# Up products grouped by width, a new first stage and a new last stage in a two-layer encoder kernel

## The chip, the cores and the metric

The kernel runs on one core of a Trainium2 chip. The metric is device time in microseconds (us) from the start to the end of one execution. Three runs of the kernel before gave a median of 789.08 us (788.89 to 789.4).

## The reference, cut to what matters

The input is x, 256 tokens by 1024 channels, and there are two layers. Each layer does this:

```
xn = rms_norm(x);  h = xn @ w_in                  # 6176 columns
ya = conv_module(...)       # "glu" columns: gated unit, depthwise conv of 31 taps, LayerNorm, swish
yb = gla_branch(...)        # "gvl": values and low-rank gates; "qk"; "gr"
yc = attention_branch(...)  # "att": windowed attention with rotary and a sink
yd = pool_branch(...)       # "pin": mean pooling of widths 2, 4, 8, 16
merged = sum_n sigmoid(gate_n) * (y_n @ w_branch_n)
x = x + merged @ w_out
x = x + square(relu(rms_norm(x) @ w_ffn_up)) @ w_ffn_down     # 1024 -> 4096 -> 1024
...
return rms_norm(x, final_norm_g)
```

The norms are not applied ahead of the products. Each channel's gain is multiplied into x when it is split, and the token's factor R (one over the root mean square) is multiplied in behind the products, when their sums are read.

## The kernel before, in words

All products run with operands of type float32r, and each operand is split in two parts, hi and lo, so that hi*hi + hi*lo + lo*hi gives nearly full precision. So one product of the reference is three matrix products.

**Weights.** They come in pieces of at most 128 x 1024 numbers (512 KB), in the order that `layer_loads` writes out. `fetch(i)` issues a piece's transfer into one of three `raw` buffers, on the queue of SyncE (SP). `split_w(i)` makes hi with a cast on ScalarE (ACT, L285) and lo with a subtraction on VectorE (DVE, L286), into one of five `hi` and five `lo` buffers. A raw buffer comes free when both have read it. `look_ahead` fetches up to seven pieces and splits up to four pieces ahead of the one in use.

**Order.** A planner (the tile framework's scheduler) puts each engine's instructions in a fixed order when the kernel is built. `urgent()` and `critical()` raise the priority of what stands in them; `after(t)` and `tc.issue_after(t.ins)` hold instructions back until `t` stands in the order. Each engine then works through its list in that order.

**First stage, layer 0.** x arrives with channels on partitions, in four pairs of channel tiles (256 KB each), in turn with the first four weight pieces, all on SP (L933 to L938). `split_x` makes hi (ACT, L437) and lo (DVE, L438) of each channel tile. The first products are `gvl` (8 channel tiles by 288 columns, two token tiles, 48 products of 288 columns), then `glu1` and `glu0` (96 products of 256 columns), then `qk`. `Stats` squares x and sums it, and `st.finish` makes R, which `gla_in` needs to read the `gvl` sums out of their two PSUM banks. `WARM` products on a tile of ones stand ahead of all.

**MLP.** `up(c)` makes 256 hidden channels: for each of 8 channel tiles and two halves t it issues a product of 512 columns (hi weights by x's hi and lo side by side, L1158) and one of 256 columns (lo weights by x's hi, L1159). `down(c)` multiplies the hidden channels back, 24 products of 512 columns (L329 to L331). `up(c)` and `down(c - 1)` take turns, and 16 blocks of each make a layer.

**Layer switch.** When the last two blocks of `down` have made the first half of the channels (h = 0), `add_mlp` adds it to x (DVE, L1210). `turn_x` turns x with PE transposes (L447) and splits it for the next layer's products.

**Last stage, layer 1.** When a token tile `it` is complete, its sum of squares gives one over the root, o and e, and `dg` is that factor on a diagonal (L1279). `normed(it)` multiplies x by the diagonal, which turns and scales it at once (L1244, 8 products of 128 columns in full float32, two passes each), multiplies by the final gain (L1245 on DVE, L1248 on ACT) and sends it out in two transfers.

Of the kernel before, what the change touches and what calls it, by code (L numbers as in the profile page):

```python
# [30 lines left out]
GVL_CUTS = (((0, 2), (2, 4), (4, 6), (6, 8)), ((0, 1), (1, 3), (3, 6), (6, 8)))  # L31
CONV_V = 18
WARM = 14
# [17 lines left out]
def layer_loads(first):  # L51
# [17 lines left out]
    for i, (a, b) in enumerate(cuts):  # L69
        if not first and a == 4:  # L70
            cols256("glu1", C_GLU + 256, (0,))
            cols256("glu0", C_GLU, (0,))
        add(("gvl", i), "w_in", a, b, gvl)
    if first:
        cols256("glu1", C_GLU + 256)
        cols256("glu0", C_GLU)
    else:
        cols256("glu1", C_GLU + 256, (1,))
        cols256("glu0", C_GLU, (1,))
# [47 lines left out]
def cst_layout():  # L127
    off = 0
    for name, n in (("ident", 128), ("band", 256), ("lev", 160), ("rope", 32), ("cnt", 512), ("o64", 128)):
        CST[name] = (off, n)  # L130
        off += n
    return off
# [40 lines left out]
def trunk_kernel(ctx: ExitStack, tc: tile.TileContext, x, w, prm, wup, poolw, cst, out, depth, dbg=None):  # L173
# [49 lines left out]
    cst_t = sb.tile([P, NCST], F32, name="cst_t")  # L223
# [5 lines left out]
    ident = cs("ident")  # L229
# [40 lines left out]
    def fetch(i):  # L270
# [4 lines left out]
        raws[i] = r  # L275
        return d

    def split_w(i):
# [5 lines left out]
        with urgent():  # L284
            a = S.copy(h[:, :n], r[:, :n])  # L285
            V.tensor_tensor(lo[:, :n], r[:, :n], h[:, :n].bitcast(F32), ALU.subtract)  # L286
# [22 lines left out]
    nc.scalar.dma_start(prm_t, prm)  # L309
# [617 lines left out]
    for l in range(depth):  # L927
        if l == 0:
# [4 lines left out]
            for f in range(4):  # L933
                nc.sync.dma_start(xT[:, 2 * f : 2 * f + 2, :], x[:, 2 * f : 2 * f + 2, :])
                sent = fetch(f)
                last = split_w(f)
                for t in (2 * f, 2 * f + 1):
                    split_x(xh[:, t, :], xl[:, t, :], xT[:, t, :], gain0[:, t : t + 1])  # L938
            state["raw"] = state["next"] = 4
            st = Stats()  # L940
            for f in range(4):
                with urgent(), tc.issue_after(last.ins):
                    st.add(f, xT)
# [3 lines left out]
        if l == 0:  # L947
            state["raw"] = 5
            with tc.issue_after(fetch(4).ins):
                nc.sync.dma_start(cst_t, cst)  # L950
            G.tensor_copy(o64r, o64)
        (nc.sync if l else nc.scalar).dma_start(wup_t, wup[:, l * 256 : l * 256 + 256])
        nc.sync.dma_start(poolw_t, poolw[:, l * 256 : l * 256 + 256])
# [18 lines left out]

        cuts = list(enumerate(GVL_CUTS[l == 0]))
        for i, (k0, k1) in cuts if l == 0 else cuts[:2]:
# [4 lines left out]
        ps_g, ps_a = mmt(), None  # L979
        if l:  # L980
            ps_a = mmt()
# [13 lines left out]
        for i in range(2) if l == 0 else (1,):  # L995
            part256(ps_g, "glu1", i)
        if l == 0:
            ps_a = mmt()
        for i in range(2) if l == 0 else (1,):
            done = part256(ps_a, "glu0", i)  # L1000
# [144 lines left out]
        ups = {}  # L1145

        def up(c, parts=(0, 1)):
# [3 lines left out]
            for i in parts:  # L1151
                wh, wl = piece(l, (("up", c), i))
                for k in range(4):
                    f = fx[i][:, k]
                    for t in range(2):
                        w1 = slice(t * P, (t + 1) * P)
                        first, last = i + k == 0, (i, k) == (1, 3)
                        mm(ps[t], wh[:, k, w1], f, start=first, stop=False, skip_group_check=True)  # L1158
                        done = mm(  # L1159
                            ps[t][:, 0, :], wl[:, k, w1], f[:, 0, :], start=False, stop=last, skip_group_check=True  # L1160
                        )
            if 1 not in parts:
# [12 lines left out]
            hid[c] = (hh, hl)  # L1175

# [11 lines left out]

        for i in range(2):
            for c in range(2):  # L1190
                with after(turned if (i, c) == (0, 1) else None):
                    done = up(c, (i,))
                if (i, c) == (0, 0):
                    turned = turn_x(f_parts, 1, col(l, 8, 8), done)
# [18 lines left out]
        if nxt < depth:  # L1213
# [6 lines left out]
            for h in range(2):  # L1220
                for c in (14, 15):
                    with after(turned if (c, h) == (15, 1) else None):
                        done = down(c, (0, 1), (h,))
                    if (c, h) == (14, 1):
                        turned = turn_x(x_parts, 0, col(nxt, 0, 8), done)
# [5 lines left out]
        else:  # L1231
# [4 lines left out]
            def normed(it):  # L1236

                with urgent():
                    for h in range(2):
                        ps = mmt((P, 4, P))  # L1240
                        yo = gh_p.tile([P, 4, P], F32, tag="gh", name=nm("yo"))
                        for t in range(4):
                            c = (4 * h + t) * P
                            mm(ps[:, t, :], xt[:, it, c : c + P], dgs[it], start=True, stop=True)  # L1244
                        V.tensor_tensor(yo[:, :2], ps[:, :2], gb[:, 4 * h : 4 * h + 2], ALU.mult)  # L1245
                        for t in (2, 3):
                            kt = 4 * h + t
                            S.activation(yo[:, t, :], ps[:, t, :], AF.Copy, scale=g[:, kt : kt + 1])  # L1248
                        (nc.sync, nc.scalar)[h].dma_start(
                            out[:, 4 * h : 4 * h + 4, it * P : (it + 1) * P], yo  # L1250
                        )

            dgs = []
            for it in range(2):
                for h in range(2):
                    for c in (14, 15):
                        done = down(c, (it,), (h,))
                    if (it, h) == (1, 0):
                        with tc.issue_after(done.ins):
# [103 lines left out]
```

## Time and profile before

| | |
|---|---|
| median of 3 runs | 789.08 us (788.89 to 789.4) |
| the profiled execution's own time | 788.53 us |
| its span, first to last instruction | 786.7 us |
| PE (TensorE) busy | 773.7 us, 98%, 4298 matrix products |
| DVE busy | 585.3 us, 74% |
| ACT busy | 476.0 us, 61% |
| moved by DMA | 138.49 MB, mean 176 GB/s |

A busy PE is not a PE at its peak: the records of consecutive products overlap, so that the distance from one product's start to the next one's start (its pitch) tells what a product costs. The 1.83 us between the span and the execution's own time lie around the span and are not touched by the kernel's order.

### The profile page before, as it was taken

Reading aid. Unit: us, or ns where it says so; the run is one execution under the profiler, and the core shown is the slowest. Engines: PE = TensorE matmul, PEld = TensorE weight load, DVE = VectorE, ACT = ScalarE, POOL = GpSimd, SP = SyncE. Lnnn points to the kernel's source line nnn. Section 1 sums busy time; section 2 is a strip of 40 time slices with the busy share of each in tenths; the row PEclk is TensorE's granted clock in tenths of the full one; section 3 lists DMA queues with packets and bytes.
Section 4 is the critical chain, followed back from the end, with each engine's and each line's share of the span. In section 5 each row is a group of like instructions: output and inputs, shape, how many; then the busy total and the mean of one; then the engine's idle time right before and its main releaser. Section 6 shows DMA issues by size and latency. Waiting matters only on the chain.

```text
span 786.7 us, 11413 instructions
## 1 busy us (share of the span) xinstructions
PE 773.7 (98%) x4298; PEld 657.8 (84%) x4298; DVE 585.3 (74%) x863; ACT 476.0 (61%) x740; POOL 9.7 (1%) x22
## 2 busy tenths in 40 slices
PE   8999999999999999999999999999999999999996
PEld 7998888888888888888799988788888888888885
DVE  6789999888676666666677999978776766666653
ACT  6788895854564444444568787858545644444443
POOL 2000000000000000000000000000000000000000
PEclk9999999999999999999999999999999999999999
DMA  8755545455556555555465564346655576665631
GB/s 282 234 167 174 176 138 157 140 190 179 188 165 207 191 188 188 190 187 192 141 190 182 161 211 159 108 135 165 209 171 178 165 212 189 190 192 191 193 113 53
DMA packets 41126, 138.49 MB, mean 176 GB/s; under 512 B 4528, under 2 KB 7280, under 8 KB 41072
## 3 DMA queue, kind: packets, MB, share of 16 engines
q1 hardware_dynamic: 39616, 137.05, 55.1%
q10 hardware_dynamic: 1456, 0.73, 0.3%
q8 instruction: 33, 0.54, 0.3%
q14 instruction: 21, 0.17, 0.1%
HBM read 136.71 MB, written 1.05 MB: 175 GB/s over the span
## 4 chain that ended last, share of the span: by engine, by line
PE 95%; DVE 2%; DMA 1%; issue 1%; ACT 1%; DVEq 0%
PE mm L1158 15%; PE mm L329 11%; PE mm L330 10%; PE mm L331 10%; PE ax L331 9%; PE ax L329 9%; PE ax L330 9%; PE mm L1159 8%; PE mm L322 2%; PE mm L321 2%; PE mm L320 2%; PE ax L661 1%; PE ax L822 1%; PE ax L447 1%; DMA raw<-in_w_dram 1%
## 5 line engine op out<-in xcount | busy, mean ns | idle before, releaser
L286 DVE TENSOR_TENSOR lo<-raw,hi 128x1024 fp32r<-128x1024 f32 (+2 forms) x260 | 314.5, 1209 | 139.3 <-ACT hi L285 137.7
L285 ACT CAST hi<-raw 128x1024 fp32r<-128x1024 f32 (+2 forms) x260 | 269.6, 1038 | 210.1 <-issue 53.8
L1158 PE MATMUL mm<-fx,hi 128*128 128x512 f32 x512 | 181.9, 398 | 0.0
L1159 PE MATMUL mm<-fx,lo 128*128 128x256 f32 x512 | 143.1, 281 | 0.0
L329 PE MATMUL mm<-hi,xh 128*128 128x512 f32 (+1 forms) x320 | 122.1, 384 | 1.0 <-ACT hi L285 1.0
L330 PE MATMUL mm<-lo,xh 128*128 128x512 f32 (+1 forms) x320 | 122.3, 383 | 0.4 <-DVE lo L286 0.4
L331 PE MATMUL mm<-hi,xl 128*128 128x512 f32 (+1 forms) x320 | 120.6, 381 | 0.0
L1158 PEld LDWEIGHTS mm<-fx,hi 128*128 128x128 f32 x512 | 96.0, 188 | 23.2 <-DVE fx L438 0.3
L329 PE MATMUL ax<-hi,hh 128*128 128x512 f32 x256 | 100.0, 391 | 0.0
L330 PE MATMUL ax<-lo,hh 128*128 128x512 f32 x256 | 99.9, 390 | 0.0
L1159 PEld LDWEIGHTS mm<-fx,lo 128*128 128x128 f32 x512 | 96.6, 189 | 1.8 <-DVE lo L286 0.3
L331 PE MATMUL ax<-hi,hl 128*128 128x512 f32 x256 | 97.1, 389 | 0.0
L329 PEld LDWEIGHTS mm<-hi,xh 128*128 128x128 f32 x320 | 59.8, 188 | 12.5 <-ACT hi L285 1.2
L330 PEld LDWEIGHTS mm<-lo,xh 128*128 128x128 f32 x320 | 60.1, 188 | 11.3 <-DVE lo L286 0.8
L331 PEld LDWEIGHTS mm<-hi,xl 128*128 128x128 f32 x320 | 60.1, 188 | 11.1
L329 PEld LDWEIGHTS ax<-hi,hh 128*128 128x128 f32 x256 | 48.0, 188 | 10.6
L331 PEld LDWEIGHTS ax<-hi,hl 128*128 128x128 f32 x256 | 48.1, 188 | 10.2
L330 PEld LDWEIGHTS ax<-lo,hh 128*128 128x128 f32 x256 | 48.1, 188 | 8.9
L1170 ACT COPY t<-mm 128x256 f32<-128x256 f32 x64 | 23.4, 370 | 46.0 <-PE mm L1159 46.0
L322 PE MATMUL mm<-xh,lo 128*128 128x256 f32 x160 | 45.5, 284 | 1.0 <-DVE lo L286 1.0
L321 PE MATMUL mm<-xl,hi 128*128 128x256 f32 x160 | 45.4, 284 | 0.0
L320 PE MATMUL mm<-xh,hi 128*128 128x256 f32 x160 | 45.2, 284 | 0.0
(264 smaller groups left out, 983.3 us busy)
## 6 DMA issues: line engine op xcount, KB each, us to landing
raw<-in_w_dram SPq DMA_DIRECT2D x252, 512.0 KB, 3.6
raw<-in_w_dram SPq DMA_DIRECT2D x6, 288.0 KB, 3.2
xT<-in_x_dram SPq DMA_DIRECT2D x4, 256.0 KB, 4.5
cst_t<-in_cst_dram SPq DMA_DIRECT2D x1, 608.0 KB, 5.2
out_dram<-yo SPq DMA_DIRECT2D x2, 256.0 KB, 2.4
out_dram<-yo ACTq DMA_DIRECT2D x2, 256.0 KB, 2.4
raw<-in_w_dram SPq DMA_DIRECT2D x1, 432.0 KB, 4.3
poolw_t<-in_poolw_dram SPq DMA_DIRECT2D x2, 128.0 KB, 4.6
```

What stands on the lines that cost most here:

```text
L285: a = S.copy(h[:, :n], r[:, :n])
L286: V.tensor_tensor(lo[:, :n], r[:, :n], h[:, :n].bitcast(F32), ALU.subtract)
L320: mm(o, a, xh[:, kx, :], start=start, stop=False, skip_group_check=True)
L321: mm(o, a, xl[:, kx, :], start=False, stop=False, skip_group_check=True)
L322: return mm(o, b, xh[:, kx, :], start=False, stop=stop, skip_group_check=True)
L329: mm(o, xh[:, kx, tk], wh[:, k, :], start=start, stop=False)
L330: mm(o, xh[:, kx, tk], wl[:, k, :], start=False, stop=False)
L331: return mm(o, xl[:, kx, tk], wh[:, k, :], start=False, stop=stop)
L447: last = nc.tensor.transpose(ps[:, t, it * P : (it + 1) * P], src[:, it, c : c + P], ident)
L1158: mm(ps[t], wh[:, k, w1], f, start=first, stop=False, skip_group_check=True)
L1159: done = mm(ps[t][:, 0, :], wl[:, k, w1], f[:, 0, :], start=False, stop=last, skip_group_check=True)
L1170: S.copy(z[:, t, :], ps[t][:, 1, :])
```

## The change

Four places are changed.

1. **Up products.** In `up`, the two products of 512 columns of a channel tile now stand together, and then the two of 256 columns. `up` also returns its last product, and the first four part blocks of `up` in a layer are chained in order with `after`.
2. **First stage.** `gvl` comes in pieces of 1, 1, 2, 3 and 1 channel tiles, and `glu` comes in pieces of two channel tiles by 512 columns; the products take turns (gvl 0, gvl 1, glu 0, gvl 2, glu 1, gvl 3, gvl 4, then glu 2 and glu 3 behind R's users). x's first pair comes on SP with pieces 0, 1 and 2; the second pair is issued on ACT's queue behind the cast of piece 1, the third and the fourth behind the cast of piece 4. The `glu` piece 0 is split in two halves. `WARM` goes from 14 to 11. The identity becomes a tile of its own, fetched with `prm_t` and `wup_t` behind piece 5; the other constants and `poolw_t` come later still.
3. **Layer switch.** The first `turn_x` for the next layer stands behind half of the last `down` block (the first token tile) instead of ahead of all of it, and the other half stands behind the transposes.
4. **Last stage.** x is turned by plain transposes against the identity (`turned_out`) and multiplied by the gain when it is read out; the token factor comes as a row from one product of ones with `dg` and is multiplied in afterwards (`normed`). Token tile 0's transposes stand between the `down` products of token tile 1. Token tile 1 goes out in four transfers on two queues.

```
 def split_w(i, cuts=1):
...
+            for c in range(cuts):
+                p = slice(c * n // cuts, (c + 1) * n // cuts)
+                a = S.copy(h[:, p], r[:, p])
+                V.tensor_tensor(lo[:, p], r[:, p], h[:, p].bitcast(F32), ALU.subtract)
...
-            for f in range(4):
-                nc.sync.dma_start(xT[:, 2 * f : 2 * f + 2, :], x[:, 2 * f : 2 * f + 2, :])
-                sent = fetch(f)
-                last = split_w(f)
-                for t in (2 * f, 2 * f + 1):
-                    split_x(xh[:, t, :], xl[:, t, :], xT[:, t, :], gain0[:, t : t + 1])
-            state["raw"] = state["next"] = 4
+            sent = last = None
+            for f, pieces in enumerate(((0, 1, 2), (3, 4), (), ())):
+                with after(last if f >= 2 else sent), critical():
+                    (nc.scalar if f else nc.sync).dma_start(
+                        xT[:, 2 * f : 2 * f + 2, :], x[:, 2 * f : 2 * f + 2, :]
+                    )
+                tiles = (2 * f, 2 * f + 1)
+                for i in pieces:
+                    fetch(i)
+                    if i == 0:
+                        split_x(xh[:, 0, :], xl[:, 0, :], xT[:, 0, :], gain0[:, 0:1])
+                        sent = split_w(0)
+                        split_x(xh[:, 1, :], xl[:, 1, :], xT[:, 1, :], gain0[:, 1:2])
+                        continue
+                    if i == pieces[0]:
+                        for t in tiles:
+                            split_x(xh[:, t, :], xl[:, t, :], xT[:, t, :], gain0[:, t : t + 1])
+                    last = split_w(i, 2 if i == 2 else 1)
+                    if i != 2:
+                        sent = last
+                if not pieces:
+                    for t in tiles:
+                        with tc.issue_after(sent.ins):
+                            split_x(xh[:, t, :], xl[:, t, :], xT[:, t, :], gain0[:, t : t + 1])
+            state["next"] = 5
...
-            with tc.issue_after(fetch(4).ins):
-                nc.sync.dma_start(cst_t, cst)
+            with tc.issue_after(fetch(5).ins):
+                nc.sync.dma_start(ident, cst[:, CST["ident"][0] :])
+                nc.sync.dma_start(prm_t, prm)
+                nc.sync.dma_start(wup_t, wup[:, :256])
...
+        if l == 0:
+            ps_g, ps_a = mmt(), mmt()
+            for i, (k0, k1) in cuts:
+                gvl(i, k0, k1)
+                if i in (1, 2):
+                    glu(i - 1)
...
         if l == 0:
-            ps_a = mmt()
+            for i in (2, 3):
+                done = glu(i)
+            with tc.issue_after(state["dma"].ins):
+                nc.sync.dma_start(cst_t, cst[:, : NCST - P])
+                nc.sync.dma_start(poolw_t, poolw[:, :256])
...
                     for t in range(2):
                         w1 = slice(t * P, (t + 1) * P)
-                        first, last = i + k == 0, (i, k) == (1, 3)
                         mm(ps[t], wh[:, k, w1], f, start=first, stop=False, skip_group_check=True)
+                    for t in range(2):
+                        w1 = slice(t * P, (t + 1) * P)
                         done = mm(
                             ps[t][:, 0, :], wl[:, k, w1], f[:, 0, :], start=False, stop=last, skip_group_check=True
                         )
...
+                done = down(14, (0, 1), (h,))
+                if h == 0:
+                    down(15, (0, 1), (h,))
+                else:
+                    with after(done):
+                        done = down(15, (0,), (h,))
+                    turned = turn_x(x_parts, 0, col(nxt, 0, 8), done)
+                    with after(turned):
+                        down(15, (1,), (h,))
...
+            def turned_out(it, h, behind=None):
+                ps = mmt((P, 4, P))
+                yo = gh_p.tile([P, 4, P], F32, tag="gh", name=nm("yo"))
+                for t in range(4):
+                    c = (4 * h + t) * P
+                    last = nc.tensor.transpose(ps[:, t, :], xt[:, it, c : c + P], ident)
...                                              # read out times the gain: ACT for (0, 1), else DVE
+            def normed(it, dg):
+                rb = axt((P, P))
+                last = mm(rb, ones, dg, start=True, stop=True)
+                rbb = rb.unsqueeze(1).broadcast_to([P, 4, P])
+                for h in range(2):
+                    yo = yos.pop((it, h))
+                    V.tensor_tensor(yo, yo, rbb, ALU.mult)
+                    for n, t in enumerate((0, 2)):
+                        (nc.sync, nc.scalar)[n if it else 0].dma_start(
+                            out[:, 4 * h + t : 4 * h + t + 2, it * P : (it + 1) * P], yo[:, t : t + 2]
                         )
```

## Rows read from the trace of the kernel before

**Rows 1.** The page, chain of work that ended last: shares of the span by engine.

```profile
PE 95%; DVE 2%; DMA 1%; issue 1%; ACT 1%; DVEq 0%
```

**Rows 2.** Waits of PE: us in total, times, longest us.

```profile
PE mm L329 <- DVE merged L1086: 1.0, 1, 1.0
```

**Rows 3.** Timeline of PE in an up block: start us, us, engine, line, out<-in, shape.

```profile
299.69 0.40 PE L1158 MATMUL mm<-fx,hi 128*128 128x512 f32 x1
...
302.87 0.40 PE L329 MATMUL ax<-hi,hh 128*128 128x512 f32 x1
```

**Rows 4.** Timeline of PE in a down block, products of 512 columns throughout.

```profile
699.70 0.39 PE L331 MATMUL ax<-hi,hl 128*128 128x512 f32 x1
...
702.87 0.39 PE L330 MATMUL ax<-lo,hh 128*128 128x512 f32 x1
```

**Rows 5.** Timeline of PE where four products of 256 columns meet three of 512.

```profile
95.21 0.29 PE L622 MATMUL ax<-t,qs 128*128 128x256 f32 x1
...
96.39 0.29 PE L622 MATMUL ax<-t,qs 128*128 128x256 f32 x1
```

**Rows 6.** Timeline of PE in the first stage.

```profile
1.03 4.99 PE L314 MATMUL warm<-ones 128*128 128x128 f32 x28 [1.03 <-DVE ones L237]
...
5.78 0.51 PE L329 MATMUL mm<-hi,xh 128*128 128x288 f32 x2
...
15.76 0.38 PE L322 MATMUL mm<-xh,lo 128*128 128x256 f32 x1 [1.03 <-DVE lo L286]
...
16.81 0.28 PE L321 MATMUL mm<-xl,hi 128*128 128x256 f32 x1
...
18.01 0.28 PE L322 MATMUL mm<-xh,lo 128*128 128x256 f32 x1
...
28.50 0.36 PE L320 MATMUL mm<-xh,hi 128*128 128x256 f32 x1
```

**Rows 7.** Timeline of ACT and DVE in the first stage.

```profile
4.12 0.91 ACT L437 ACTIVATE xh<-xT,gain 128x256 fp32r<-128x256 f32 x2 [1.19 <-DMA gain<-in_prm_dram]
...
13.07 1.04 ACT L285 CAST hi<-raw 128x1024 fp32r<-128x1024 f32 x1
...
15.62 0.41 DVE L369 TENSOR_TENSOR sums<-t 128x256 f32<-128x256 f32 x1
...
24.57 0.42 DVE L354 SCALAR_TENSOR_TENSOR R<-t,R 128x258 f32<-128x258 f32 x1
...
26.12 0.68 DVE L506 TENSOR_TENSOR t<-mm,R 128x512 f32<-128x512 f32 x1
```

**Rows 8.** The page, DMA issues: count, KB each, median us from issue to landing.

```profile
raw<-in_w_dram SPq DMA_DIRECT2D x252, 512.0 KB, 3.6
...
xT<-in_x_dram SPq DMA_DIRECT2D x4, 256.0 KB, 4.5
```

**Rows 9.** Timeline of DVE and PE at the layer switch.

```profile
388.56 1.40 DVE L1210 SCALAR_TENSOR_TENSOR xt<-ax,r,xt 128x512 f32<-128x512 f32 x2
...
389.36 0.33 PE L447 MATMUL ax<-cst_t,xt 128*128 128x128 f32 x1 [0.39 <-DVE xt L1210]
...
390.01 0.98 PE L447 MATMUL ax<-cst_t,xt 128*128 128x128 f32 x7 [0.33 <-DVE xt L1210]
...
391.68 0.88 DVE L438 SCALAR_TENSOR_TENSOR xl<-ax,prm_t,xh 128x256 fp32r<-128x256 f32 x2 [0.37 <-ACT xh L437]
```

**Rows 10.** The chain in order of time, 0 to 60 us: plain transposes of x.

```profile
56.80 1.75 PE ax L1029 x16
```

**Rows 11.** Timeline of DVE and ACT's queue in the last stage.

```profile
775.61 0.75 DVE L1210 SCALAR_TENSOR_TENSOR xt<-ax,r,xt 128x512 f32<-128x512 f32 x1
...
778.37 0.42 DVE L1245 TENSOR_TENSOR yo<-mm,prm_t 128x256 f32<-128x256 f32 x1 [0.96 <-PE mm L1244]
...
779.60 0.34 DVE L1279 TENSOR_SCALAR t<-cst_t,rt,re 128x128 f32<-128x128 f32 x1
...
783.26 0.40 ACTq L1249 DMA_DIRECT2D out_dram<-yo  x1
```

More of the change, by code (lines that the diff above doesn't have):

```diff
@@ L73, in layer_loads @@
         add(("gvl", i), "w_in", a, b, gvl)
+        if first and i in (1, 2):
+            cols512("glu", "w_in", C_GLU, (i - 1,))
     if first:
-        cols256("glu1", C_GLU + 256)
-        cols256("glu0", C_GLU)
+        cols512("glu", "w_in", C_GLU, (2, 3))
     else:
@@ L128, in cst_layout @@
     off = 0
[L129 removed]
+    for name, n in (("band", 256), ("lev", 160), ("rope", 32), ("cnt", 512), ("o64", 128), ("ident", 128)):
         CST[name] = (off, n)
@@ L227, in cs @@
         return cst_t[:, off : off + n]
-    ident = cs("ident")
+    ident = sb.tile([P, P], F32, name="ident")
     band = cs("band").rearrange("p (a j) -> p a j", a=2)
@@ L1234, in trunk_kernel @@
             gb = g.unsqueeze(2).broadcast_to([P, KD, P])
[L1236 to L1250, printed above, removed]
+            yos = {}
@@ new lines, in turned_out @@
+            def turned_out(it, h, behind=None):
[4 more added lines that the diff above has]
+                    last = nc.tensor.transpose(ps[:, t, :], xt[:, it, c : c + P], ident)
+                if (it, h) == (0, 1):
+                    for t in range(4):
+                        S.activation(yo[:, t, :], ps[:, t, :], AF.Copy, scale=g[:, 4 + t : 5 + t])
+                else:
+                    for t in (0, 2):
+                        with after(behind):
+                            V.tensor_tensor(
+                                yo[:, t : t + 2], ps[:, t : t + 2], gb[:, 4 * h + t : 4 * h + t + 2], ALU.mult
+                            )
+                yos[it, h] = yo
+                return last
@@ L1251, in normed @@
                         )
+                return last
             dgs = []
+            done = None
             for it in range(2):
@@ L1256, in trunk_kernel @@
                     for c in (14, 15):
-                        done = down(c, (it,), (h,))
+                        with after(done if it else None):
+                            done = down(c, (it,), (h,))
+                        if (it, h, c) == (1, 0, 14):
+                            with tc.issue_after(done.ins), urgent():
+                                for n in range(2):
+                                    last = turned_out(0, n)
+                            done = last
                     if (it, h) == (1, 0):
-                        with tc.issue_after(done.ins):
-                            normed(0)
+                        with tc.issue_after(done.ins), urgent():
+                            last = normed(0, dgs[0])
+                        done = last
                     add_mlp(it, h)
```

64 lines of the change are left out of this document (36 added, 28 removed).

## The prediction

> **What bounds the kernel now.** I read the chain of waits first: 95% of it is PE [rows 1], so nearly all of the time is a row of products, and what counts is the pitch of that row and the few places where it stops. Then I read the waits of PE and its timeline. In the middle there is one stop of a microsecond, where a product waits for DVE's merging of a branch [rows 2]. The other stops lie where this change works: in the first stage [rows 6], at the layer switch [rows 9] and behind the last product [rows 11]. So I cost four places one by one, and take the long rest as it is, shifted.
>
> **Up products.** Nine pairs of 512 and 256 columns fill 302.87 - 299.69 = 3.18 us, 353 ns a pair [rows 3]. In a run of equal widths a product of 512 columns takes 3.17 us / 14 = 226 to 227 ns [rows 4], and one of 256 takes 1.20 us / 10 = 120 ns (from 16.81 to 18.01) [rows 6]. These make 347 ns, so going from one width to the other and back costs 6.7 ns. The edit halves the number of such goings: four products now take 707 ns, and would take 693 if a change of width cost nothing. But it isn't said that one going there and back costs the same behind two products as behind one. The nearest row has four of 256 between three of 512: 1.18 us [rows 5], where the run pitches make 4 x 120 + 3 x 227 = 1.16, so a going there and back costs 20 ns there. Between one in a row (6.7 ns) and four in a row (20 ns), two in a row come to about 11 by a straight line: 693 + 11 = 704 ns, 2.2 ns less than now. There are 16 blocks x 8 channel tiles x 2 layers = 256 such fours, so the term is 0.6 us. The bounds are a gain of 3.4 us (13.3 ns each, no cost of changing) and a loss of 1.7 us (20 ns each). The second sums come a little later, but the reading of an up block lies beside 24 products of `down`, 24 x 227 = 5.4 us. I cost that at nothing; if that cover were gone it would be one reading of two products' length, 0.2 us a block.
>
> The Trainium skill speaks against this edit: "TensorE: Matmul & The Clock Gate", section Back-to-back issue gap, gives a warm matmul N/2.4 + 2.5 ns by its own columns, whatever stands beside it, which for one pair is about 325 ns in either order (an estimate from that page of the Trainium skill). Here a pair takes 353 ns and the neighbours matter by 6.7 [rows 3, 4, 6]; by that section of the Trainium skill this term would be zero.
>
> **First stage.** PE's first real product starts at 5.78 and `qk` starts at 28.50 [rows 6], 22.7 us. The products between are 96 of 256 columns at 120 ns = 11.5 us and 48 of 288 columns; from 227 ns and 120 ns a column costs 0.42 ns, so one of 288 is 133 ns (an estimate), 6.4 us in all. That is 17.9; R's own products take some 0.9 (an estimate from six passes at up to 0.2). About 3.9 us are stops, such as that at 15.76 for a lo [rows 6].
>
> Afterwards: x's first pair still lands at 4.1 [rows 7]; one split of 256 columns is 0.46 (half of 0.91) and the cast of piece 0 is about the same, so the first product can go at 5.0. The products of ones stand in the way less: 28 passes fill until the first real product [rows 6], and 22 remain, some 1.0 us less. Start 5.0, 0.8 earlier.
>
> Then x comes in turn. The second pair is issued behind the cast of piece 1, two splits and one cast after 5.0, at 5.9. From issue to landing took 4.5 us for x, and 3.6 for a piece in the long run [rows 8]; with less in flight than before I hold both ends open. With 4.5 it lands at 10.4, and with 0.46 + 0.65 for its split and piece 3's cast (an estimate between 0.46 for 256 columns and 1.04 for 1024 [rows 7]) its first product goes at 11.5. Until then PE has 12 products of 133 and 24 of 120 ns = 4.5 us, with lo waits about until 10.2. A stop of 1.3. The next 4.5 us (gvl 2, glu 1) with a lo wait of 0.5 go until 16.5. Piece 4's cast ends at 11.5 + 1.04 = 12.5; behind it pairs three and four are issued (0.4 each) and land at 17.0 and 17.4; first product 17.5, a stop of 1.0. Then 24 x 133 + 48 x 120 ns = 9.0, and R's 0.9: 27.4, a gain of 1.1. With 3.6 the same steps give 10.6, then 15.6, pairs landing at 15.2 and 15.6, a first product at 15.7, and 25.5, a gain of 3.0. I lean to x's own row, from this stage, and hold 1.8. What is late next is R: it ends at 24.99 now [rows 7], and its sums will wait for a pair of x that lands at 15.6 to 17.4. From there its steps are a split, a square, two additions, R's products and five steps of 0.4, shortest about 6 us (an estimate from the lengths in rows 7), with a cast or two in front 8 to 9: 24 to 26. `qk` needs a bank that is read behind it. I take off 0.3 and use 1.5. ACT issues three transfers of x: three times 0.4, the 0.4 at pair two delaying `glu` piece 0's cast, counted in the lo waits. SP's `ident`, `prm_t` and `wup_t` behind piece 5 cost three issues of 0.4 while piece 6 waits for a raw buffer anyway; without that wait it would be 1.2 us on piece 6, of 0.8 us of products. The constants sent later are first needed behind the turning of x at 56.80 [rows 10] and land by about 42; that is the cover of this move.
>
> **Layer switch.** The adds end at 388.56 + 1.40 = 389.96, and two transposes wait for them. The first stands idle for 0.39 behind a record that runs 0.39 - 0.23 = 0.16 past its pitch [rows 4, 9], so it is 0.55 late; the next comes 0.65 behind it where such a run has 1.75 / 16 = 0.11 [rows 9, 10], 0.54 more. In all 1.1 us. With six `down` products (6 x 227 = 1.36 us) put ahead, the transposes come at 388.8 + 1.36 = 390.2, behind the adds: all of it goes. Late next is the split: the first products of the next layer then start 0.9 + 1.36 after 390.2, at 392.4. lo of the first two channel tiles is made from 391.68 to 392.56 [rows 9]; the second is used six products later. It fits by 0.3; without that cover up to 0.5 would come back. I take 1.1; the bounds are 0.3 and 1.2.
>
> **Last stage.** The last add starts at 775.61 behind the last product [rows 11], and the span ends at 786.7, 11.1 us later; the last transfer is issued at 783.26, so 3.4 us from issue to end. `dg` is ready at 779.94, behind two readings of token tile 0 of 0.42 that stand ahead of its steps on DVE; without them it would be 779.1. DVE will have readings of token tile 1 to do, but these can stand in the gaps where it waits for ACT. Then come one product of ones (0.4 with its latency, an estimate) and two multiplications of 512 columns at 0.68 [rows 7], so the last issue is at about 780.9 and the end at 784.3: 2.4 less. On the other side, ahead of the last `down` product now stand eight transposes at 0.11 (0.9), a product of ones in two passes (0.2) and some 0.2 of changing over, 1.3 us which PE cannot hide. Net 1.1; the bounds are 0.2 (two readings in front of `dg` as now) and 2.0 (half of the transposes in a wait).
>
> **The sum.** 0.6 + 1.5 + 1.1 + 1.1 = 4.3 us from the profiled execution's 788.53: 784.2. The median of the runs is 0.55 above that execution, so 784.8. A change below 0.2%, 1.6 us, cannot be told from none.
>
> **The rivals.**
> A: as summed, 784.8 (783.4 to 786.5): 42%.
> B: changing width costs nothing once it is rarer, the up term is 3.4: 782.0. The run pitches speak for it, the four in a row [rows 5] against it: 12%.
> C: a product's pitch is its own affair in any order, the four take 707 ns as now: 785.4. For it: the cost per product of 256 is 5 ns in rows 5 and 6.7 in rows 3, hardly a difference. That section of the Trainium skill would have it so. 16%.
> D: the first stage doesn't do what it should, since each pair of x comes a full 4.5 us behind a cast and stops move rather than go: 786.3, and up to 787.5 with a second late cast: 14%.
> E: the planner orders the middle anew and makes two more stops like that of rows 2, 1.3 us each with the restart (an estimate): 787.4: 8%.
> F, slower: R is late. From its sums (15.62 + 0.41) to its end are 9.0 us now [rows 7], though the steps between are some 3: the rest is waiting in line. If the sums end at 22 and these 9.0 us stay, R comes at 31, and with a cast and two readings of the bank ahead of it `qk` starts at 33.1 where it now starts at 28.5. The stage then loses 4.6 instead of gaining 1.5: 790.9. The sign turns where `qk` starts 2.8 late, the gain of the other three places, so with R at about 29. Against it: now nobody waits for R, so that its place in the lines tells nothing of how early it could come. 8%.
>
> **Numbers.** Faster by over 0.2% (below 787.5): A, B, C, most of D and a part of E, 0.84. Within 0.2%: 0.09. Slower: 0.07, from F and a little of E. The range goes from 781.7, just below B, to 787.7, just above E; outside are F, and of B and E less than half each, under 2 in 10.
>
> **What would show it.** The pitch of four products in an up block: 704 ns, against 693 (B) or 707 (C). `qk`'s first product at about 27.0, with stops ahead of gvl 2 and gvl 3, and R before 27; R behind 31 is F. No wait ahead of the transposes at the layer switch. From the last add to the end 8.6 us instead of 11.1, and eight transposes between the last products. The prediction is wrong where the pitch moves by more than 10 ns a four, or where the next wait in the middle grows by what the stages ahead of it gained.

## The result, and the profile after

The changed kernel takes 793.58 us (median of 4 runs, 793.11 to 794.47) where the kernel before takes 789.16 beside it (788.89 to 789.40). The ratio is 1.0056, 95% interval [1.0041, 1.0071]: slower by 4.4 us, where 4.3 us faster was predicted. The profiled execution took 794.47 us, its span is 792.7. It lies 0.9 us above its median and the profiled execution of the kernel before 0.6 below its own, so the two traces are 6.0 us apart and not 4.4.

To see where the time went I set the same products of both traces side by side. Each figure is the distance between the starts of two products in PE's timeline (the last row ends at the span's end), in us:

| stretch | before | after | difference |
|---|---|---|---|
| start to the first product of the branches' output, layer 0 | 188.83 | 199.06 | +10.2 |
| first to last `up` product, layer 0 / layer 1 | 167.66 / 167.61 | 166.38 / 166.28 | -1.3 / -1.3 |
| last `up` to last `down` product, layer 0 | 12.85 | 11.73 | -1.1 |
| last `down` product to the next layer's first output product | 179.41 | 180.16 | +0.75 |
| last `up` to last `down` product, layer 1 | 10.79 | 12.05 | +1.3 |
| last `down` product to the end | 11.53 | 8.99 | -2.5 |

From the first output product to the first `up` product, the only stretch left out, it is 24.0 us in each layer of both. All of the loss lies in the first row, which has only the first stage of the edit in it: of its 10.2 us, 7.7 lie ahead of `qk`'s first product (36.19, before 28.50) and 2.5 behind it. The waits of PE name the stop (us in total, times, longest us), beside the one of [rows 2], which is still there:

```profile
PE mm L323 <- DVE t L509: 8.1, 1, 8.1
...
PE mm L332 <- DVE merged L1128: 1.0, 1, 1.0
```

PE's timeline in the first stage answers to [rows 6]. The first product starts at 5.00, as predicted. The last product of `glu` starts at 27.85, about as before (28.27), and then PE stands idle until 36.19, where `qk` starts:

```profile
5.00 0.40 PE L332 MATMUL mm<-hi,xh 128*128 128x288 f32 x1
...
16.44 0.53 PE L332 MATMUL mm<-hi,xh 128*128 128x288 f32 x2 [0.93 <-ACT xh L440]
...
24.77 0.50 PE L378 MATMUL ax<-onesd,sums 128*128 128x1 f32 x4
...
27.85 0.28 PE L325 MATMUL mm<-xh,lo 128*128 128x256 f32 x1
36.19 0.55 PE L323 MATMUL mm<-xh,hi 128*128 128x256 f32 x1 [8.07 <-DVE t L509]
```

ACT in the same stretch, and below it DVE, answer to [rows 7]. The reader is to follow one chain through them. ACT stands 2.56 us for x's third pair, then casts on. The sums start at 21.59, 6 us later than before. R's own products stand on PE behind products of `glu` and end at 25.27 (L378), when the cast of 23.94 is over; R's Ln (L352) stands behind the next cast, of 26.47, which waits for a transfer of weights, its Exp behind one more, and on DVE R's last step (L357) stands behind a lo. So R ends at 33.2, and the reading of `glu`'s bank (L509), behind another lo, at 36.0. From the end of the sums to the end of R it is 11.2 us, where it was 9.0.

```profile
15.88 0.91 ACT L440 ACTIVATE xh<-xT,gain 128x256 fp32r<-128x256 f32 x2 [2.56 <-DMA xT<-in_x_dram]
...
23.94 1.05 ACT L289 CAST hi<-raw 128x1024 fp32r<-128x1024 f32 x1 [1.98 <-DMA raw<-in_w_dram]
26.47 1.05 ACT L289 CAST hi<-raw 128x1024 fp32r<-128x1024 f32 x1 [1.48 <-DMA raw<-in_w_dram]
27.42 0.47 ACT L352 ACTIVATE R<-ax,epsd 128x258 f32<-128x258 f32 x1
27.88 1.05 ACT L289 CAST hi<-raw 128x1024 fp32r<-128x1024 f32 x1
28.83 0.41 ACT L353 ACTIVATE R<-R 128x258 f32<-128x258 f32 x1
```

```profile
21.59 0.42 DVE L372 TENSOR_TENSOR sums<-t 128x256 f32<-128x256 f32 x1
...
31.66 1.23 DVE L290 TENSOR_TENSOR lo<-raw,hi 128x1024 fp32r<-128x1024 f32 x1 [0.68 <-ACT hi L289]
32.80 0.42 DVE L357 SCALAR_TENSOR_TENSOR R<-t,R 128x258 f32<-128x258 f32 x1
34.15 1.23 DVE L290 TENSOR_TENSOR lo<-raw,hi 128x1024 fp32r<-128x1024 f32 x1 [0.93 <-ACT hi L289]
35.29 0.16 DVE L1028 TENSOR_SCALAR Rh<-R 128x2 f32<-128x2 f32 x1
35.36 0.68 DVE L509 TENSOR_TENSOR t<-mm,R 128x512 f32<-128x512 f32 x1
```

The kernel before had much of this waiting already. On PE and ACT:

```profile
18.80 0.50 PE L375 MATMUL ax<-onesd,sums 128*128 128x1 f32 x4
...
20.42 1.05 ACT L285 CAST hi<-raw 128x1024 fp32r<-128x1024 f32 x1 [2.47 <-DMA raw<-in_w_dram]
21.37 0.47 ACT L349 ACTIVATE R<-ax,epsd 128x258 f32<-128x258 f32 x1
```

From the end of the sums to R's products it was 2.3 us there and is 2.3 now; from the end of R's products to Ln it was 2.1, behind a cast that waited for weights, and is 2.1 now. What is new is that the sums come 6.0 us later, and that the steps from Ln on take 2.2 us more. Before, `qk` still had `glu`'s products ahead of it when R was done; now they are over.

The stop has a second price. In the busy times by stretch (the figure after the five engines is the granted clock) PE's clock falls to half in it, to the 1.2 GHz level, and is still there while `qk` and what follows run:

```profile
28.00:31.00 3.00, 0.13 (x2) 0.00 (x0) 2.77 (x4) 1.66 (x3) 0.00 (x0) 1.00 0.64 209
31.00:36.00 5.00, 0.00 (x0) 0.00 (x0) 3.42 (x6) 3.54 (x5) 0.00 (x0) 0.52 0.77 258
36.00:41.00 5.00, 4.81 (x22) 4.83 (x23) 2.62 (x7) 0.79 (x2) 0.29 (x1) 0.50 0.73 249
41.00:45.00 4.00, 4.00 (x33) 3.99 (x32) 1.65 (x3) 2.04 (x4) 0.00 (x0) 0.95 0.01 4
```

The other three places. In an up block, beside [rows 3], five fours of products go from 298.01 to 301.49: 3.48 us, 696 ns a four:

```profile
298.01 0.63 PE L1201 MATMUL mm<-fx,hi 128*128 128x512 f32 x2
298.48 0.39 PE L1204 MATMUL mm<-fx,lo 128*128 128x256 f32 x2
...
301.49 0.40 PE L332 MATMUL ax<-hi,hh 128*128 128x512 f32 x1
```

At the layer switch, beside [rows 9], the eight transposes run without a stop, but the next layer's first product starts 0.53 us behind the last `down` product and not 0.23:

```profile
399.13 1.08 PE L450 MATMUL ax<-ident,xt 128*128 128x128 f32 x8
399.97 0.48 PE L332 MATMUL ax<-hi,hh 128*128 128x512 f32 x1
...
401.21 0.40 PE L334 MATMUL ax<-hi,hl 128*128 128x512 f32 x1
401.74 0.40 PE L332 MATMUL mm<-hi,xh 128*128 128x288 f32 x1
```

Its xh, on ACT, stands behind three squares of the norm's sums (399.38, 400.00, 400.61; before, two stood ahead of it). Of the 0.75 us that come back, 0.3 lie there, and 0.35 in front of the first product with xl, which starts 1.10 us behind that product and not 0.75:

```profile
400.61 0.62 ACT L397 ACTIVATE t<-xt 128x512 f32<-128x512 f32 x1
...
401.23 0.82 ACT L440 ACTIVATE xh<-ax,prm_t 128x256 fp32r<-128x256 f32 x2
```

In the last stage, beside [rows 11], the readings of the last transposes (L1303) fill DVE's gaps between the last add and the diagonal `t` (L1357), which is ready at 787.20, 3.1 us behind the start of the last add (before, 4.3 us); the last multiplication ends at 789.06:

```profile
784.13 0.75 DVE L1258 SCALAR_TENSOR_TENSOR xt<-ax,r,xt 128x512 f32<-128x512 f32 x1 [0.98 <-PE ax L334]
784.80 0.75 DVE L1303 TENSOR_TENSOR yo<-mm,prm_t 128x256 f32<-128x256 f32 x2
...
786.85 0.35 DVE L1357 TENSOR_SCALAR t<-ident,rt,re 128x128 f32<-128x128 f32 x1
787.77 1.29 DVE L1316 TENSOR_TENSOR yo<-yo,ax 128x512 f32<-128x512 f32 x2 [0.58 <-PE ax L1312]
```

### The profile page after: what moved, and what is told of

The parts are those of the page before. It is cut to its first block, busy times and chain, and to the rows that moved or that the text cites. A ratio compares the mean times of both kernels' runs of the same rounds, so it can differ in the third digit from the quotient of the medians.

```text
span 792.7 us, 11391 instructions
## 1 busy us (share of the span) xinstructions
PE 772.3 (97%) x4280; PEld 657.3 (83%) x4280; DVE 586.2 (74%) x871; ACT 475.5 (60%) x738; POOL 7.8 (1%) x22
## 4 chain that ended last, share of the span: by engine, by line
PE 93%; DMA 3%; DVE 2%; ACT 1%; issue 0%; DVEq 0%; SPq 0%; ACTq 0%
PE mm L1201 15%; PE mm L332 10%; PE mm L334 10%; PE mm L333 10%; PE ax L334 9%; PE ax L332 9%; PE ax L333 9%; PE mm L1204 7%; DMA raw<-in_w_dram 2%; PE mm L323 2%; PE mm L324 2%; PE mm L325 2%; PE ax L664 1%; PE ax L825 1%; DVE lo L290 1%; ACT hi L289 1%
## 5 line engine op out<-in xcount | busy, mean ns | idle before, releaser
L290 DVE TENSOR_TENSOR lo<-raw,hi 128x1024 fp32r<-128x1024 f32 (+1 forms) x262 | 314.4, 1201 | 163.6 <-ACT hi L289 162.3
L289 ACT CAST hi<-raw 128x1024 fp32r<-128x1024 f32 (+1 forms) x262 | 269.9, 1032 | 259.4 <-PE mm L1201 85.8
L1201 PE MATMUL mm<-fx,hi 128*128 128x512 f32 x512 | 162.1, 396 | 0.0
L1204 PE MATMUL mm<-fx,lo 128*128 128x256 f32 x512 | 103.3, 278 | 0.0
L1201 PEld LDWEIGHTS mm<-fx,hi 128*128 128x128 f32 x512 | 81.3, 189 | 3.8
L323 PEld LDWEIGHTS mm<-xh,hi 128*128 128x128 f32 x160 | 31.6, 198 | 9.9 <-issue 8.2
```

The costliest lines, as they stand in the source:

```text
L289: a = S.copy(h[:, p], r[:, p])
L290: V.tensor_tensor(lo[:, p], r[:, p], h[:, p].bitcast(F32), ALU.subtract)
L323: mm(o, a, xh[:, kx, :], start=start, stop=False, skip_group_check=True)
L1204: done = mm(ps[t][:, 0, :], wl[:, k, w1], f[:, 0, :], start=False, stop=last, skip_group_check=True)
```

## The experiments

Times are medians; the kernel before stood at 788.96 to 789.34 us beside them.

**The parts taken alone.** e1 has the old first stage and the other three parts new; e2 only the new order of `up`, e3 only the new last stage, e4 only the new first stage. The edits are those of the diff above.

> The change without its first stage: up products by width, layer switch and last stage as changed, the first stage as before. Theory S (the whole loss is made in the first stage, the rest gained what the two traces show, 2.6 for up, 0.4 to 1.1 for the switch and 1.3 at the end): 784.2 to 785.0. Rival M (the new order costs in the middle too, and the gain of the other parts is given back there): 787 or more.

> The kernel before with the up products by width alone. Theory S: two times 1.3 less, 786.5, and a pitch of about 697 ns for four products against 707. Rival (what the prediction held): 704 ns, 788.5. Rival (width doesn't matter): 789.1.

> The kernel before with the new last stage alone. Theory S: from the last up product to the end 1.3 less than before, 787.8. Rival (the transposes ahead of the last down products cost as much as the end gains): 789.1.

> The kernel before with the new first stage alone. Theory S: the first product of qk starts at about 36 instead of 28.5 and the granted clock falls for some 10 us behind it; 10 more than before, 799. Rival M (the first stage alone costs less, part of the loss comes from its meeting the other parts): 792 to 795.

| run | us | ratio to before, 95% interval |
|---|---|---|
| e1, without the first stage | 785.06 | 0.9944 [0.9930, 0.9957] |
| e2, `up` alone | 786.47 | 0.9964 [0.9952, 0.9977] |
| e3, last stage alone | 787.73 | 0.9979 [0.9969, 0.9988] |
| e4, first stage alone | 797.81 | 1.0105 [1.0091, 1.0118] |

e1 gains 4.1 us and e4 loses 8.6; together that is 4.5, about the 4.4 that the whole loses. The first stage alone loses, and without it the change is a gain. That this gain is nearly the 4.3 us predicted for all four parts is chance: for these three 2.8 were predicted.

**The layer switch alone (e11).** e2 and e3 gain 2.7 and 1.45 us, which leaves nothing of e1's 4.1 for the switch.

```diff
-                for c in (14, 15):
-                    with after(turned if (c, h) == (15, 1) else None):
-                        done = down(c, (0, 1), (h,))
...
+                    with after(done):
+                        done = down(15, (0,), (h,))
+                    turned = turn_x(x_parts, 0, col(nxt, 0, 8), done)
+                    with after(turned):
+                        down(15, (1,), (h,))
```

> The kernel before with the new order at the layer switch alone (the eight transposes behind one group of the last down step, not ahead of both). The prediction's term: 1.1 us gained and kept, 787.9 to 788.1 us. Theory 'given back', from the traces of the runs with the switch in them (last down product 1.1 us earlier, but from there to layer 1's first output product 180.1 us and not 179.4): about 0.4 us gained, 788.5 to 788.8 us, the gvl products behind the transposes waiting for xh and xl, which have only six products ahead of them and not twelve.

788.96 against 789.34, ratio 0.9997 [0.9988, 1.0006]: no difference that can be told, and 1.1 us (0.9986) is outside the interval, while the 0.35 us that the traces leave are inside. In its trace the last `down` product comes 1.1 us earlier, and from there to layer 1's first output product it is 180.18 us where it was 179.41. What PE no longer waits for ahead of the transposes it mostly waits for behind them.

**PE's wait filled (e7).**

```diff
+            idle = axt((P, P))
+            with tc.issue_after(done.ins), critical():
+                for n in range(32):
+                    done = mm(idle, ones, ones, start=True, stop=True)
```

> The changed kernel, with 32 products of a tile of ones (128 columns, read by nobody) added behind the last product of glu, in TensorE's stop before qk. Theory 'clock': the granted clock then stays at 1.0 past qk's start, its 256-column products take 120 ns and not 213, which gives back about 2 us: 791 to 792 us, with qk's first product still at 36. Rival: the clock's fall costs nothing on the path that sets the end, 793 to 794 us.

791.36 us, ratio 1.0029 [1.0017, 1.0041], 2.2 us below the changed kernel. Products that nobody reads fill the wait, `qk` starts 0.5 us earlier only, the granted clock stays at 1.00 from 28 to 45 us, and `qk`'s products are at their 120 ns at once:

```profile
27.42 7.30 PE L1039 MATMUL ax<-ones 128*128 128x128 f32 x64
35.69 0.36 PE L323 MATMUL mm<-xh,hi 128*128 128x256 f32 x1 [0.96 <-DVE t L509]
35.88 0.28 PE L324 MATMUL mm<-xl,hi 128*128 128x256 f32 x1
36.00 0.28 PE L325 MATMUL mm<-xh,lo 128*128 128x256 f32 x1
```

From `qk`'s first product to the first output product it is 160.3 us in the kernel before, 162.9 in the changed kernel and 160.2 here. So some 2 us of the loss is the clock (1.7 by the medians, which are 2.2 apart with 0.5 of it ahead of `qk`; 2.7 by these traces), and the rest is the stop itself.

**Another bank for `qk` (e6).**

```diff
-        ps = mmt()
+        ps = (bank or mmt)()
...
-        ps_qk = pair256(l, "qk", xs)
+        ps_qk = pair256(l, "qk", xs, axt if l == 0 else mmt)
```

> The changed kernel, with the product qk of layer 0 written to a PSUM bank of the other pool, so that it need not wait until conv_in has read the banks of glu. Theory 'bank': the stop of 8.1 us was only for the bank; qk starts at about 28 right behind glu, the granted clock stays at 1.0, and the total falls by 5 to 8 us to 786 to 788.5 us. Theory 'R': whatever follows needs R as well, so the stop moves behind qk, its 12 products fill only part of it, and the total falls by 2 to 4 us, to 789.5 to 791.5 us. Rival 'neither': the other pool's bank is missed elsewhere by the same amount, 793 us or more.

794.18 us, ratio 1.0065 [1.0050, 1.0080], no gain. The order that the planner made put a product of 512 columns first, and this waits for the same reading of the bank:

```profile
PE mm L332 <- DVE t L509: 7.7, 1, 7.7
```

So it doesn't tell what a `qk` that is free of that bank would give, nor whether the stop can be mended there.

**x's pairs at the start (e5).**

```diff
-                with after(last if f >= 2 else sent), critical():
+                with critical():
```

> The changed kernel, with x's second to fourth pairs issued at the start from ACT's queue instead of in turn behind casts. Theory 'x late': ACT's stop of 2.6 us for x's third pair goes, the casts behind it and the sums come about 2.5 us earlier, R finishes at about 30 instead of 33.2 and qk's first product at about 33 instead of 36.2; total about 790.5 us. Rival 'same bytes': the three pairs now share the transfers with the first pieces of weights, glu finishes 2 us later than 27.9, R is still queued behind the casts of the tenth to thirteenth pieces and finishes within 1 us of 33.2; total 793 to 795 us.

787.93 us, ratio 0.9982 [0.9973, 0.9992]: 5.6 us below the changed kernel, more than expected. Its trace is of an execution of 791.49 us, 3.6 above the median, and is read for the order of work alone: R's Ln now stands behind one waiting cast and R ends at 30.3, though `gain`, pushed behind three transfers, holds the first product back to 9.71.

**R written early, casts held loosely (e8).**

```diff
-        with urgent():
+        with urgent(), after(state.get("hold") if 9 <= i <= 13 else None):
...
+                if i == 3:
+                    with urgent():
+                        R = st.finish()
+                    state["hold"] = st.done
```

> The changed kernel, with the steps of R written ahead of the fourth gvl step, and the casts of the tenth to fourteenth pieces allowed only behind R's last operation on ACT (in the order that results, the casts of the tenth and eleventh piece still stand ahead of R's Ln, and one cast between Ln and Exp). Theory 'R behind casts': R finishes 3 to 4 us earlier, at 29 to 30, qk starts at 32 to 33, total 789 to 790.5 us. Rival 'pieces late': the casts held back make the last glu pieces late instead, glu finishes after 30, and the total stays at 792 to 795 us.

792.77 us, ratio 1.0047 [1.0032, 1.0062], 0.8 below the changed kernel. R ends 1.7 us earlier, at 31.5, but three los whose casts had been made stand between it and the reading of the bank, which starts at 34.86:

```profile
31.04 0.43 DVE L357 SCALAR_TENSOR_TENSOR R<-t,R 128x258 f32<-128x258 f32 x1
31.39 3.49 DVE L290 TENSOR_TENSOR lo<-raw,hi 128x1024 fp32r<-128x1024 f32 x3
...
34.86 0.69 DVE L509 TENSOR_TENSOR t<-mm,R 128x512 f32<-128x512 f32 x1
```

R came earlier, by less than the 3 to 4 us expected, and weights queued between it and the reading. The time is the rival's, but not by its way: the last product of `glu` starts at 28.37, not after 30.

**x early, with R ahead of two casts or behind them (e9, e10).** Both issue x's pairs early, e9 behind the transfer of `gain`, e10 behind ACT's loading of its table; what differs in the order that results is mostly R's place. The diff is e9's; in e10 `gained` is the instruction of the second line.

```diff
-    nc.scalar.dma_start(gain0, prm[:, :KD])
-    S.preload_act_table_set(LN_EXP)
+    gained = nc.scalar.dma_start(gain0, prm[:, :KD])
+    S.preload_act_table_set(LN_EXP)
...
-                with after(last if f >= 2 else sent), critical():
+                with after(gained if f else None), critical():
```

> As e5, but the three x pairs are issued behind the transfer of gain, which e5 had pushed behind them (first product at 9.7 instead of 5.0). In the order that results, R's Ln and Exp stand on ACT ahead of two casts that stood ahead of them in e5's profile or the changed kernel. Theory 'x late, and R behind casts': first product back at about 5, R finishes by 27 to 28, qk's first product by 30 to 31, no stretch at a clock of 0.5; total 785 to 787 us. Rival 'weights set the pace': with R early the last glu piece and the pieces behind it are late instead (raw transfers), first product of the output stage still 5 us later than in the kernel before, total 788 to 790 us.

> As e9, but the three x pairs are issued behind the loading of ACT's table too; x still lands early, but in the order that results four casts stand ahead of R's Ln (two in e9), one between Ln and Exp and two more ahead of v. This differs from e9 in hardly more than R's place among the casts. If the casts ahead of R set the time, R finishes 3 to 5 us later than in e9 and the total is 2 to 4 us above e9's; if x's transfers alone do, both are within 1 us of each other.

e9 takes 786.18 us, ratio 0.9966 [0.9952, 0.9980]; e10 791.73, ratio 1.0035 [1.0023, 1.0047], 5.5 us above e9 and so more than the 2 to 4 expected. The sums start at about the same time (19.52 and 19.21). In e9's rows, ACT's and then DVE's, Ln follows the cast of 22.66 and R ends at 27.5:

```profile
22.66 1.05 ACT L289 CAST hi<-raw 128x1024 fp32r<-128x1024 f32 x1 [3.19 <-DMA raw<-in_w_dram]
23.61 0.47 ACT L352 ACTIVATE R<-ax,epsd 128x258 f32<-128x258 f32 x1
24.11 0.42 ACT L353 ACTIVATE R<-R 128x258 f32<-128x258 f32 x1
...
27.04 0.42 DVE L357 SCALAR_TENSOR_TENSOR R<-t,R 128x258 f32<-128x258 f32 x1
...
29.18 0.68 DVE L509 TENSOR_TENSOR t<-mm,R 128x512 f32<-128x512 f32 x1
```

In e10 Ln stands behind one cast more and Exp behind another, R ends at 31.1, and the stop is back:

```profile
24.96 1.05 ACT L289 CAST hi<-raw 128x1024 fp32r<-128x1024 f32 x1 [1.40 <-DMA raw<-in_w_dram]
25.92 0.47 ACT L352 ACTIVATE R<-ax,epsd 128x258 f32<-128x258 f32 x1
26.29 1.05 ACT L289 CAST hi<-raw 128x1024 fp32r<-128x1024 f32 x1
27.22 0.42 ACT L353 ACTIVATE R<-R 128x258 f32<-128x258 f32 x1
```

PE's waits in e10:

```profile
PE mm L323 <- DVE t L509: 5.3, 1, 5.3
```

So x early takes only 1.9 us off the changed kernel while R stays behind the casts (e10), and 5.5 more go where R comes ahead of them (e9). e9's first product was expected at 5 and came at 7.31: the load of ACT's table that stands ahead of x's split comes at 3.94 (in e10 at 1.16, with the first product at 6.54), and in both runs x's second pair is split ahead of the first cast. The load written at the start comes second in e9, at 7.61.

**R ahead of the casts (e12, and e13 with x early too).** In both the casts from the ninth piece on are held behind R's Exp, which is on their own engine; e12 leaves x as the changed kernel has it, e13 adds e10's edit.

```diff
-        with urgent():
+        with urgent(), after(state.get("hold") if 8 <= i <= 13 else None):
...
-        S.activation(o, o, AF.Exp, scale=-0.5)
+        done = S.activation(o, o, AF.Exp, scale=-0.5)
...
                     st.add(f, xT)
+            with urgent():
+                R = st.finish()
+            state["hold"] = st.done
```

> The changed kernel, x's pairs in turn as it has them, but R's steps written right behind the sums, and the casts of the ninth piece on held back on ACT until behind R's Exp. In the order that results, Ln and Exp stand ahead of the three casts that stood ahead of Ln in the changed kernel and of the one between Ln and Exp. Theory 'casts ahead of R': with the sums at 22 as before, Ln follows by 24, R finishes at 26 to 28 though x is as late as it was, TensorE's long stop shrinks from 8 to 1 to 2 us, no long stretch at a clock of 0.5; total 785.5 to 788 us. Rival 'x late': R can't come before about 30, or the casts held back make the next stop in its place; total 790 us or more.

> Both: x's pairs early as in e10 (one load of ACT's table) and R ahead of the ninth piece's cast as in e12. R finishes by 24 to 25, the first product starts at 5 to 6, no stop before qk; 784 to 785.5 us if the second load of the table and R's place are all that keeps e9 at 786.2. Rival 'weights set the pace': stops for raw pieces take their place and the first stage is no shorter than the old one; 785.5 to 787 us.

e12 takes 790.19 us, ratio 1.0012 [1.0003, 1.0021]; e13 786.81, ratio 0.9968 [0.9958, 0.9977]. In e12 no cast stands ahead of Ln any more and R ends at 28.1, but ACT now idles 4.78 us in front of Ln, since the sums end at 21.50 and R's own products (L379) stand behind products of `glu` in PE's list and end at 24.65:

```profile
24.69 0.48 ACT L352 ACTIVATE R<-ax,epsd 128x258 f32<-128x258 f32 x1 [4.78 <-PE ax L379]
25.20 0.42 ACT L353 ACTIVATE R<-R 128x258 f32<-128x258 f32 x1
```

Beside the changed kernel's 793.58: casts out of R's way alone 3.4 us (e12), x early alone 1.9 (e10), both 6.8 (e13) and 7.4 (e9). So each of the two gives something alone. Together they give 1.5 us more than the sum of e12 and e10, which speaks for their making each other worse, but is not far outside the scatter of these runs. The times of e12 and e13 are those of their rivals, by the theories they should have been 2 and 1 us lower. In e12 the casts held back do make the next stop: no wait for L509 is left, but 2.8 us of waits for casts, and the transfers move 132 GB/s between 20 and 30 us where they moved 214 in the changed kernel. Two more losses are in these traces. In e12 the granted clock is 0.79 and 0.64 in the stretches from 25 to 28 and 28 to 31 us, around that stop. And from 60 to 200 us PE stands idle for 2.6 us in e12 and 2.0 in e13, where it is 0.3 in the changed kernel, in stops of 0.3 to 1.2 us. So by these runs R's place is the larger part of the cause, and it can't be had for nothing by holding casts.

## Why the prediction was wrong

**First stage: the step that failed.** The term was a gain of 1.5 us; measured alone it is a loss of 8.6. Its start (5.00), the stop for x (0.93 at 16.44; 1.0 was reckoned at 17.5) and the end of the `glu` pieces were about right: 27.85, where the steps with x's own transfer time gave 27.4. That end is partly luck: the stop of 1.3 us reckoned ahead of gvl 2 did not come, and waits for casts of weights (0.52 at 7.67, 0.61 at 20.46) came in its place. What failed is the sentence on R: it "ends at 24 to 26", from "a cast or two in front", so that `qk` would start at 27. R ended at 33.2. From the landing of x's last pair 8 to 9 us were reckoned; from its split (17.51) it took 15.7, and 11.2 of these lie behind the sums, where [rows 7] had 9.0 for the same stretch. That waiting in line, for PE's list, for a cast that stands waiting for weights and for los, was left out: the casts were costed by their length, not by what they wait for. Rival F had the mechanism, and put `qk` at 33.1 where it came at 36.2; it got 8 in 100, on the ground that R's place in the lines before told nothing of how early it could come. e9, e10 and e12 show that this place decides: R at 27.5 or 28.1 and there is no stop at L509, R at 31.1 and there is one of 5.3 us.

**The clock** was in no step. In the stop of 8 us it falls to half, for about ten us, which costs some 2 us (e7).

**Up.** A gain of 0.6 us was predicted, with bounds of +3.4 and -1.7. The stretches give 1.28 + 1.33 = 2.6, and e2 as a whole 2.7. A four takes 696 ns, not 704; that is 11 less than before, just beyond the 10 that the prediction named as its sign of being wrong, and nearer to rival B's 693. The step that was mis-sized is the price of a going between widths. It came from setting an up block's pairs against pitches of other blocks: 227 ns from a `down` block, 120 from the first stage, and the 20 ns of [rows 5]. The up blocks have pitches of their own. These are the mean distances between the starts of two products there, in ns, over PE's timeline of both layers:

| columns of the two | before | after |
|---|---|---|
| 512, then 512 | | 234 |
| 512, then 256 | 236 | 233 |
| 256, then 256 | | 115 |
| 256, then 512 | 117 | 117 |

In the new order a product costs nearly the same whichever width follows it, so that a going there and back costs about 1 ns. The four gets cheaper since each product does, those of 512 by some 3 ns and those of 256 by some 2. Why is not shown: the new order also writes two banks of PSUM (the memory that takes the products) in turn, where the old one wrote one bank twice running, and no run separates this from the widths. Rival C has no gain here, and the 9 to 11 ns a four speak against it. They speak against the section Back-to-back issue gap of the Trainium skill's "TensorE: Matmul & The Clock Gate" too, if its formula, which goes by a product's own columns and is given there for an isolated product, is taken for a stream of products.

**Layer switch.** 1.1 us was predicted; the stop went as reckoned, 1.1 us, and 0.75 came back. The prediction looked at lo ("it fits by 0.3") and not at the xh ahead of it, which ACT makes behind the squares of the sums. The bound of 0.3 us was the better value.

**Last stage.** 1.1 us was predicted and 1.45 measured (e3). Its steps hold: 1.3 us more on PE ahead of the last `down` product as reckoned, and 2.5 less behind it (2.4 was reckoned).

**In sum:** without the first stage, 0.6 + 1.1 + 1.1 = 2.8 us were predicted and 4.1 measured. The up term measured four times its size and the switch a third of its own. The sign was lost in one place.

**What stays open.** The mended first stages (e9, e13) reach the first output product at 190.12 and 191.11 us, the old one at 188.83 in the kernel before and between 188.54 and 189.86 in e1, e2, e3 and e11. So no form of the new first stage that was run beats the old one. The first product's start differs between executions of one first stage, so like is to be set beside like: the old one has 5.78 in the kernel before and 6.46 to 6.63 in those four runs, the new one 5.00 in the changed kernel and 5.74 or 5.75 in e4, e6, e7, e8 and e12. e9's 7.31 is some 0.8 behind the old one's. From the first product to the first output product e9 takes 182.8 us and the old stage 182.0 to 183.2, so that e9's rest is its late start. e13 starts at 6.69, hardly late, and takes 184.4; its idle time between 60 and 200 us is 1.1 to 1.7 us more than in those runs. In both the granted clock is below 1.00 from 5 to 15 us (e9: 0.86, then 0.80 in the second half; e13: 0.74, then 0.91), where it is 1.00 in e1. An order with x early and the start of the new stage was not run. The best kernel of the study is e1, with the old first stage and the rest of the change: 785.06 us, which beats both.

## What to carry to other kernels

When a transfer is moved to a later time, follow what is computed from all of it, here the norm's factor, and count the work ahead of it on each engine with the time at which that work can start, not by its length; a result that nobody waits for today can set the stage tomorrow. When a wait goes, look at the next consumer's whole line on its engine (here squares ahead of a split) before keeping the gain. A pitch is to be taken from the block that is changed, not from another. And judge parts apart: gains of 4.1 us lay hidden under one loss of 8.6.

## What the runs showed of the hardware

An idle time of 8 us on PE in the first stage was followed by a granted clock of 0.50 to 0.52 from 31 to 41 us, with products of 256 columns at 213 ns and not 120; with products of ones in the wait the granted clock stayed at 1.00 in the same stretch. A shorter stop was followed by a fall too: in e12, where PE waits 1.95 us up to 26.60, the granted clock is 0.64 from 28 to 31 us.

The other surprise is that a product's cost depends on its block: 512 columns take 227 ns in a `down` block and 233 to 236 in an up block, 256 columns 120 ns in the first stage and 115 to 117 in an up block. In the up block the order of the products moves each of them by 2 to 3 ns, and 512, 512, 256, 256 is 9 to 11 ns cheaper than 512, 256, 512, 256.
